# One inverse product for two heads in a chunked RWKV-7 chain, and output rows finished one by one

## The chip, the core and the metric

The kernel runs on one core of a Trainium2 chip. The metric is the device time of one execution in microseconds (us). The profile is that of one profiled execution; its span covers the instructions that the profiler saw.

The engines are named as in the profile: PE is TensorE (matrix products), PEld its weight loads, DVE is VectorE, ACT is ScalarE, POOL is GpSimd, and SP issues most transfers. Each engine works through its own instructions in the order of the program. An instruction whose operands aren't ready holds up all that stand behind it on its engine.

## What is computed

One layer of a sequence model on 512 tokens of 1024 channels: three token mixers (a short convolution, a gated linear recurrence, and an RWKV-7 state recurrence of 16 heads of 64), merged by gates, then an MLP with a squared ReLU, and a final normalization. The part that the change touches:

```python
def step(state, inp):
    r_t, w_t, k_t, v_t, kk_t, a_t = inp
    sa = jnp.einsum('bhvk,bhk->bhv', state, -kk_t)
    state = (state * w_t[:, :, None, :]
             + sa[..., None] * (kk_t * a_t)[:, :, None, :]
             + v_t[..., None] * k_t[:, :, None, :])
    y_t = jnp.einsum('bhvk,bhk->bhv', state, r_t)
    return state, y_t
...
def rms_norm(x, g):
    xf = x.astype(jnp.float32)
    y = xf * lax.rsqrt(jnp.mean(xf * xf, axis=-1, keepdims=True) + EPS)
    return (y * g.astype(jnp.float32)).astype(x.dtype)
...
return rms_norm(x, final_g)
```

## The kernel before

All weights and activations are split into a high and a low part, and each dense product is three matrix products (`mm3`, L163 to L165, shown in the profile as `pp`, `p` and `acc`). These dense products are most of the work of PE.

The recurrence runs in 8 chunks of 64 tokens for 4 groups of 4 heads. A group goes through these steps: `krv` (projections and decays), `amat` (the matrices within a chunk, L471 and L482, tiles pA and pB), `inverse` (the inverse of a unit triangular 64x64 matrix for each of 32 pairs of head and chunk, kept as TT in the tile Z, L490 to L537), `chain` (the 8 chunks one after another, L538 to L607), and `post_norm` (the per-head normalization of the result Y, with the row transposes pYt, L627).

The four heads of a group have two numbers: h, the half of the 128 partitions of a state tile in which the head lies, and jj, the column block. `HEADS` is the order in which the (jj, h) pairs are issued. One chunk of the chain does this:

1. pu <- sv, AXt (L563): four products, one for each head. For the four heads they give the right-hand sides u0, which ACT copies from PSUM to the tile u (L566, L567).
2. pu <- u, Z (L571): four products of 64 rows, 64 columns and 64 outputs, the inverse of each head times u0. All four inverses lie in partitions 0 to 63, and so does u0.
3. py <- St, RT (L578): four 64x64 products of the carried state; not in the first chunk of a group, which has no state yet.
4. DVE copies the solution to sv (L585, L586); then come pS <- sv, BKT (L593, the new state) and py <- sv, AXt (L578, the output).

Between these dependent steps PE works on the dense projections of the next stage ("fill"). The generator functions of the chain and of the fill are woven by `weave` (L752): chain steps get a higher priority by an offset, and the scheduler then sets the final order of each engine's instructions. `pin` keeps the products of a set together. The last group has as its fill the rest of the projections and the first half of the output projection. In that group `open_m` (L807 and on) also loads earlier merge results (mh, ml) on POOL's queue.

After the four groups come the rest of the output projection, the two MLP products, and the end: `last(i)` (L973 to L999) runs the last two blocks of the second MLP product for row tile i (128 tokens, two halves of 512 channels), adds the residual (DVE, `stt`), sums the squares (ACT), multiplies by the final gain (POOL, L983), takes the square root and reciprocal, scales by it (L992 on ACT, L994 on DVE) and sends the half out. `last` is a generator with one stop before the scaling; the order of the calls is 0, 1, 2, 0, 1, 3, 3, 2, so that rows 0 and 1 are scaled after row 2's evictions, and row 2 after row 3's.

Of the kernel before, what the change touches and what calls it, by code (L numbers as in the profile page):

```python
# [9 lines left out]
F32 = mybir.dt.float32  # L10
F32R = mybir.dt.float32r
I32 = mybir.dt.int32
AF = mybir.ActivationFunctionType
# [5 lines left out]
P = 128  # L19
# [10 lines left out]
S = 512  # L30

AL, ALM = 256, 2048
D = 1024
KT = 8
NG = 4
NC = 8
L = 64
# [15 lines left out]
HEADS = ((0, 1), (0, 0), (1, 1), (1, 0))  # L53
# [40 lines left out]
def block_kernel(ctx, tc, xt, win, par, mulr, sw, wout, w1, w2, fg, cst, eyes, out):  # L94
    nc = tc.nc
    v, ac, gp, pe, sy = nc.vector, nc.scalar, nc.gpsimd, nc.tensor, nc.sync
# [4 lines left out]
    def stt(o, a, s, b, op0, op1):  # L101
        return v.scalar_tensor_tensor(out=o, in0=a, scalar=s, in1=b, op0=op0, op1=op1)  # L102
# [64 lines left out]
    def pin(first, mm):  # L167

        if first:
            tc.keep_in_program_order(mm)  # L170
# [106 lines left out]
    mld = dp.tile([6, P, S], F32R, name="mld")  # L277
    smk = sp.tile([P, S], F32, name="smk")
# [209 lines left out]
    def inverse(G_):  # L488
# [37 lines left out]
        for half in range(2):  # L526
            pg = pm.tile([P, 16, 32], F32, tag="pm", name="pT")
            for i in range(16):
                l = 16 * half + i
                pin(i == 0, pe.matmul(pg[0:32, i], gs[32:64, l], TT[32:64, l, 32:64], start=True, stop=True))  # L530
            ac.copy(TT[0:32, 16 * half:16 * half + 16, 32:64], pg[0:32])
            yield
        for h in range(2):
            ac.copy(AXt[0:64, 2 * h:2 * h + 2, :, 0],
                    G_.AR[64 * h:64 * h + 64, :, :, 0])
        G_.TT = TT
        G_.inv_done = True  # L537

    def chain(G_, c_lo, c_hi):
# [5 lines left out]
        for c in range(c_lo, c_hi):  # L545
# [19 lines left out]
            u0 = sp.tile([64, 4, L], F32, tag="u0", name="u0", bufs=1)  # L565
            ac.copy(u0[:, 0:2], pu[0:64, 0:2])  # L566
            ac.copy(u0[:, 2:4], pu[64:128, 0:2])  # L567
            yield
            for jj, h in HEADS:
                e = 2 * h + jj  # L570
                pin(e != 2, pe.matmul(pu[64 * h:64 * h + 64, 2 + jj], TT[:, e * 8 + c], u0[:, e],  # L571
                                      start=True, stop=True))
# [4 lines left out]
            def out_mm(w, x, h, jj, first, last, behind):  # L577
                mm = pe.matmul(py[64 * h:64 * h + 64, jj], w, x, start=first and jj == 0, stop=last,  # L578
                               skip_group_check=True)
                pin(behind or (jj, h) != HEADS[0], mm)  # L580

# [3 lines left out]
            v.tensor_copy(sv[0:64, 0:2], pu[0:64, 2:4])  # L585
            v.tensor_copy(sv[0:64, 2:4], pu[64:128, 2:4])  # L586
# [220 lines left out]
    G_ = GS[NG - 1]  # L807
# [101 lines left out]
    with tc.tile_pool(name="mw", bufs=2) as mw, \  # L909
# [41 lines left out]
        with tc.tile_pool(name="fin", bufs=1, side="right") as fin:  # L951
# [21 lines left out]
            def last(i):  # L973
                ss = fin.tile([P, 2], F32, tag="fss", name="fss", bufs=2)
                x3f = xr[:, i] if i < 3 else fin.tile([P, D], F32, name="x3f")
                for h in range(2):
# [6 lines left out]
                    (v if (i, h) == (3, 0) else gp).tensor_tensor(out=x3f[:, hs], in0=xr[:, i, hs], in1=fgt[:, hs], op=MUL)  # L983
                sd = fin.tile([P, 2], F32, tag="fsd", name="fsd", bufs=2)
# [3 lines left out]
                yield  # L988
                for h in range(2):
                    hs = slice(h * S, (h + 1) * S)  # L990
                    if h == 0 and i != 2:
                        ac.activation(x3f[:, hs], x3f[:, hs], AF.Copy, scale=sd[:, 0:1])  # L992
                    else:
                        v.tensor_scalar(out=x3f[:, hs], in0=x3f[:, hs], scalar1=sd[:, 0:1], scalar2=None, op0=MUL)  # L994
                    (ac if h == 0 and i != 2 else sy).dma_start(out[i, :, hs], x3f[:, hs])

            gens = [last(i) for i in range(4)]
            for i in (0, 1, 2, 0, 1, 3, 3, 2):
                next(gens[i], None)  # L999
# [75 lines left out]
```

## Time and profile before

| | us |
|---|---|
| median of 3 runs (lowest, highest) | 1125.88 (1125.72, 1127.33) |
| the profiled execution's own time | 1126.26 |
| its span | 1124.5 |
| busy: ACT | 519.2 (46%) |
| busy: POOL | 58.9 (5%) |
| first product of the chain in group 1 begins | 347.27 |
| last product of PE begins | 1114.60 |
| last output transfer issued | 1120.95 |

A row of the timeline is: start, duration, engine, line, operation, output tile <- input tiles, the tile shape on PE (rows x columns of the array), the operand's shape, and how many records are in the row. A matrix product of the types used here is two records in the profile. A square bracket at the end names the idle time before the row and what ended it. L numbers are lines of the kernel before, unless the text says otherwise; L99 to L105 are helper functions of DVE, so that tile names tell more than these lines.

### The profile page before, as it was taken

To read this page: it belongs to the slowest core of one execution; us is meant where nothing else is said; L and a number is where in the kernel's file an instruction comes from. 1 tells how busy PE (TensorE), PEld (TensorE's weight loads), DVE (VectorE), ACT (ScalarE), POOL (GpSimd) and SP (SyncE) were. 2 spreads that over 40 slices of the span, in tenths; PEclk is the share of its full clock that TensorE was granted. 3 is DMA by queue.
4 is the path that set the end of the run, shared out by engine and by line. 5 is a ranking of instruction groups with operands and counts; after the bars stand their busy time and mean duration, and the time that the engine had idled before them with its cause. 6 is when DMAs were issued, how large, how long until landed. Compare 5 with 4: busy or idle time off the path is not lost.

```text
span 1124.5 us, 16256 instructions
## 1 busy us (share of the span) xinstructions
PE 1087.3 (97%) x6396; PEld 869.7 (77%) x6396; DVE 766.3 (68%) x1369; ACT 519.2 (46%) x837; POOL 58.9 (5%) x99
## 2 busy tenths in 40 slices
PE   8899989999989999989999989999999999999996
PEld 5677867778867678867678867898888888888885
DVE  7998995989986889975888967686444443222224
ACT  6655355534457534456534474564344333112113
POOL 2200000000000000000000020100000000000003
PEclk8999997999999999999999999999999999999998
DMA  6232222231233131232231262455322225322222
GB/s 212 71 103 80 73 74 77 62 103 57 90 117 99 58 103 57 89 120 88 61 95 65 85 206 85 171 180 161 109 95 94 94 94 191 105 98 94 93 94 75
DMA packets 37772, 114.60 MB, mean 102 GB/s; under 512 B 4544, under 2 KB 8128, under 8 KB 37696
## 3 DMA queue, kind: packets, MB, share of 16 engines
q1 hardware_dynamic: 30768, 95.48, 26.6%
q0 software_dynamic: 6352, 17.30, 4.5%
q8 instruction: 50, 0.82, 0.3%
q10 hardware_dynamic: 576, 0.79, 0.2%
q14 instruction: 26, 0.21, 0.1%
HBM read 104.64 MB, written 8.91 MB: 101 GB/s over the span
## 4 chain that ended last, share of the span: by engine, by line
PE 71%; DVE 22%; issue 3%; ACT 2%; DMA 1%; SPq 0%; ACTq 0%; DVEq 0%
PE pp L163 8%; PE pp L164 8%; PE pp L165 8%; PE acc L165 6%; PE acc L164 6%; PE acc L163 6%; PE p L164 5%; PE p L165 5%; PE p L163 5%; DVE wlo L99 5%; DVE dg L99 4%; DVE Z L99 3%; PE pA L471 2%; DVE u L102 2%; PE py L578 2%
## 5 line engine op out<-in xcount | busy, mean ns | idle before, releaser
L99 DVE TENSOR_TENSOR wlo<-raw,whi 128x1024 fp32r<-128x1024 f32 (+1 forms) x172 | 209.4, 1218 | 215.7 <-ACT whi L142 213.6
L142 ACT CAST whi<-raw 128x1024 fp32r<-128x1024 f32 (+1 forms) x172 | 178.1, 1036 | 286.1 <-PE acc L165 125.7
L165 PE MATMUL pp<-hh,wlo 128*128 128x512 f32 x696 | 278.0, 401 | 5.8 <-DVE wlo L99 5.8
L164 PE MATMUL pp<-hl,whi 128*128 128x512 f32 x696 | 278.3, 400 | 3.9 <-DVE hl L102 3.9
L163 PE MATMUL pp<-hh,whi 128*128 128x512 f32 x696 | 278.5, 401 | 1.4 <-DVE ks L102 0.6
L165 PEld LDWEIGHTS pp<-hh,wlo 128*128 128x128 f32 x696 | 131.9, 190 | 34.4 <-DVE wlo L99 7.3
L163 PEld LDWEIGHTS pp<-hh,whi 128*128 128x128 f32 x696 | 132.0, 190 | 31.9 <-ACT u L664 2.1
L164 PEld LDWEIGHTS pp<-hl,whi 128*128 128x128 f32 x696 | 132.0, 190 | 31.6 <-DVE hl L102 4.7
L165 PE MATMUL p<-h2h,wlo 128*128 128x512 f32 (+1 forms) x264 | 101.2, 383 | 0.0
L163 PE MATMUL p<-h2h,whi 128*128 128x512 f32 (+1 forms) x264 | 101.1, 383 | 0.0
L164 PE MATMUL p<-h2l,whi 128*128 128x512 f32 (+1 forms) x264 | 101.0, 383 | 0.0
L163 PE MATMUL acc<-whi,ah 128*128 128x512 f32 x256 | 99.6, 389 | 0.0
L164 PE MATMUL acc<-wlo,ah 128*128 128x512 f32 x256 | 99.6, 389 | 0.0
L165 PE MATMUL acc<-whi,al 128*128 128x512 f32 x256 | 99.6, 389 | 0.0
L165 PEld LDWEIGHTS p<-h2h,wlo 128*128 128x128 f32 x264 | 49.6, 188 | 9.7
L163 PEld LDWEIGHTS p<-h2h,whi 128*128 128x128 f32 x264 | 49.6, 188 | 9.7
L164 PEld LDWEIGHTS p<-h2l,whi 128*128 128x128 f32 x264 | 49.6, 188 | 9.5
L165 PEld LDWEIGHTS acc<-whi,al 128*128 128x128 f32 x256 | 48.0, 188 | 10.1
L164 PEld LDWEIGHTS acc<-wlo,ah 128*128 128x128 f32 x256 | 48.0, 188 | 10.1
L163 PEld LDWEIGHTS acc<-whi,ah 128*128 128x128 f32 x256 | 48.0, 188 | 9.8
L99 DVE TENSOR_TENSOR Z<-Z,dg 64x31 f32<-64x31 f32 (+15 forms) x124 | 42.2, 340 | 4.1
L99 DVE TENSOR_TENSOR dg<-Z 64x31 f32<-64x31 f32 (+15 forms) x124 | 42.2, 340 | 4.1
(299 smaller groups left out, 1533.8 us busy)
## 6 DMA issues: line engine op xcount, KB each, us to landing
raw<-in_win SPq DMA_DIRECT2D x88, 512.0 KB, 3.5
raw<-in_w SPq DMA_DIRECT2D x64, 512.0 KB, 3.5
raw<-in_wout SPq DMA_DIRECT2D x16, 512.0 KB, 3.5
swr<-in_sw SPq DMA_DIRECT2D x16, 128.0 KB, 2.1
x2T<-in_xt POOLq DMA_DIRECT2D x4, 512.0 KB, 7.1
x2d<-st POOLq DMA_DIRECT2D x8, 256.0 KB, 2.6
xr<-x2d POOLq DMA_DIRECT2D x1, 2048.0 KB, 9.1
xT<-in_xt SPq DMA_DIRECT2D x3, 512.0 KB, 6.7
```

The lines of the kernel that those rows point to most:

```text
L99: return v.tensor_tensor(out=o, in0=a, in1=b, op=op)
L102: return v.scalar_tensor_tensor(out=o, in0=a, scalar=s, in1=b, op0=op0, op1=op1)
L142: ac.copy(hi[:, sl], raw[:, sl])
L163: pe.matmul(ps, wh, xh, start=start, stop=False)
L164: pe.matmul(ps, wh, xl, start=False, stop=False)
L165: pe.matmul(ps, wl, xh, start=False, stop=stop)
L471: pe.matmul(pts[h][:, ci], G_.BK[rows, jj, c], G_.AR[rows, jj, c], start=True, stop=True)
L578: mm = pe.matmul(py[64 * h:64 * h + 64, jj], w, x, start=first and jj == 0, stop=last, skip_group_check=True)
```

## The change

It has three parts.

**The inverse product.** The heads of one jj (h = 0 and h = 1) are put into one product. The inverse of h = 0 stays in partitions 0 to 63, the inverse of h = 1 is copied to partitions 64 to 127 by a transfer inside the on-chip memory on POOL's queue (64 partitions of 4 KB, one per group). The right-hand sides are written as blocks beside zeros: two tiles of 128 x 2 x 2 x 64, zeroed once at the start, take u0 of h in partitions 64h and columns 64h. A product with 128 rows, 64 outputs and 128 columns then gives both heads' solutions beside each other. Two such products for each chunk stand in place of four of 64 x 64 x 64.

**The order of heads.** `HEADS` starts with jj = 1 and puts both h of one jj next to each other; the first product of py follows it.

**The end.** The stop in `last` goes, and the four rows are called one after another. Of each row the first half is multiplied by the gain on POOL and scaled on ACT; the second half is done in one DVE instruction (x times reciprocal times gain) and sent by SP.

```diff
-HEADS = ((0, 1), (0, 0), (1, 1), (1, 0))
+HEADS = ((1, 0), (1, 1), (0, 0), (0, 1))
...
+    u0s = [sp.tile([P, 2, 2, L], F32, name=f"u0{i}") for i in range(2)]
+    for t in u0s:
+        gp.memset(t, 0.0)
...
+        Zf = Z.rearrange("p a b c -> p (a b c)")[:, 0:1024]
+        gp.dma_start(Zf[64:128].rearrange("p (l t) -> p l t", t=L), TT[:, 16:32])
...
-        G_.TT = TT
+        G_.TT = Zf.rearrange("p (j c t) -> p j c t", j=2, c=NC)
...
-            u0 = sp.tile([64, 4, L], F32, tag="u0", name="u0", bufs=1)
-            ac.copy(u0[:, 0:2], pu[0:64, 0:2])
-            ac.copy(u0[:, 2:4], pu[64:128, 0:2])
+            u0 = u0s[c % 2]
+            for h in range(2):
+                ac.copy(u0[64 * h:64 * h + 64, :, h], pu[64 * h:64 * h + 64, 0:2])
             yield
-            for jj, h in HEADS:
-                e = 2 * h + jj
-                pin(e != 2, pe.matmul(pu[64 * h:64 * h + 64, 2 + jj], TT[:, e * 8 + c], u0[:, e],
-                                      start=True, stop=True))
+            for jj in (1, 0):
+                pin(jj == 0, pe.matmul(pu[64 * jj:64 * jj + 64, 2:4].rearrange("p h v -> p (h v)"), TT[:, jj, c],
+                                       u0[:, jj].rearrange("p h v -> p (h v)"), start=True, stop=True))
...
-                mm = pe.matmul(py[64 * h:64 * h + 64, jj], w, x, start=first and jj == 0, stop=last,
+                mm = pe.matmul(py[64 * h:64 * h + 64, jj], w, x, start=first and jj == HEADS[0][0], stop=last,
...
-            v.tensor_copy(sv[0:64, 0:2], pu[0:64, 2:4])
-            v.tensor_copy(sv[0:64, 2:4], pu[64:128, 2:4])
+            for jj in range(2):
+                v.tensor_copy(sv[0:64].rearrange("p (h j) v -> p h j v", j=2)[:, :, jj], pu[64 * jj:64 * jj + 64, 2:4])
...
             def last(i):
...
-                    (v if (i, h) == (3, 0) else gp).tensor_tensor(out=x3f[:, hs], in0=xr[:, i, hs], in1=fgt[:, hs], op=MUL)
-                sd = fin.tile([P, 2], F32, tag="fsd", name="fsd", bufs=2)
+                x0, x1 = xr[:, i, 0:S], xr[:, i, S:D]
+                o0 = x0 if i < 3 else fin.tile([P, S], F32, name="x3f")
+                gp.tensor_tensor(out=o0, in0=x0, in1=fgt[:, 0:S], op=MUL)
                 tt(sd[:, 0:1], ss[:, 0:1], ss[:, 1:2], ADD)
                 ac.activation(sd[:, 1:2], sd[:, 0:1], AF.Sqrt, bias=epst[:, 0:1], scale=1.0 / D)
                 v.reciprocal(sd[:, 0:1], sd[:, 1:2])
-                yield
-                for h in range(2):
-                    hs = slice(h * S, (h + 1) * S)
-                    if h == 0 and i != 2:
-                        ac.activation(x3f[:, hs], x3f[:, hs], AF.Copy, scale=sd[:, 0:1])
-                    else:
-                        v.tensor_scalar(out=x3f[:, hs], in0=x3f[:, hs], scalar1=sd[:, 0:1], scalar2=None, op0=MUL)
-                    (ac if h == 0 and i != 2 else sy).dma_start(out[i, :, hs], x3f[:, hs])
-
-            gens = [last(i) for i in range(4)]
-            for i in (0, 1, 2, 0, 1, 3, 3, 2):
-                next(gens[i], None)
+                stt(x1, x1, sd[:, 0:1], fgt[:, S:D], MUL, MUL)
+                sy.dma_start(out[i, :, S:D], x1)
+                ac.activation(o0, o0, AF.Copy, scale=sd[:, 0:1])
+                ac.dma_start(out[i, :, 0:S], o0)
+
+            for i in range(4):
+                last(i)
```

How the scheduler now orders the engines is seen at three places. First PE in group 1, from the first chunk's right-hand sides on (L563 before, L570 after) to its inverse product (L571 before, L578 after). L163 to L165 (L164 to L166 after) are fill.

```order
L563 MATMUL pu<-sv,AXt 64x64 x4
L164 MATMUL pp<-hl,whi 128x512
L165 MATMUL pp<-hh,wlo 128x512
L163 MATMUL pp<-hh,whi 128x512
L571 MATMUL pu<-u_3078,Z 64x64 x4
```

Now there are twelve fill products between them in place of three:

```order
L570 MATMUL pu<-sv,AXt 64x64 x4
L165 MATMUL pp<-hl,whi 128x512
L166 MATMUL pp<-hh,wlo 128x512
L164 MATMUL pp<-hh,whi 128x512
L165 MATMUL pp<-hl,whi 128x512
L166 MATMUL pp<-hh,wlo 128x512
L164 MATMUL pp<-hh,whi 128x512
L165 MATMUL pp<-hl,whi 128x512
L166 MATMUL pp<-hh,wlo 128x512
L164 MATMUL pp<-hh,whi 128x512
L165 MATMUL pp<-hl,whi 128x512
L166 MATMUL pp<-hh,wlo 128x512
```

The next rows are one fill product and the new inverse product, `L578 ... 64x128 x2`. The same nine products more stand at this place in all four groups, and are missing from the fill later in the chain: in the last group 22 products fewer stand ahead of the first pYt.

Second, PE at the next chunk of the same group, which has a carried state: the inverse product and what follows it, before.

```order
L571 MATMUL pu<-u_3135,Z 64x64 x4
L578 MATMUL py<-St,RT 64x64 x4
L404 MATMUL pn<-bh,bd 128x512
L550 MATMUL pV<-ident,v_1510 128x128
L550 MATMUL pV<-ident,v_1511 128x128
```

And the same place in the changed kernel:

```order
L408 MATMUL pn<-bh,bd 128x512
L578 MATMUL pu<-u_221,Z 64x128 x2
L585 MATMUL py<-St,RT 64x64 x4
L557 MATMUL pV<-ident,v_1512 128x128
L557 MATMUL pV<-ident,v_1513 128x128
```

The state's products still follow the inverse product directly, but the two sets no longer have the same tile shape on the array: 128 rows x 64 columns, then 64 x 64.

Third, DVE at the end of the kernel, before: `xr<-acc` are evictions, `fsd<-fss` sums the two halves' squares, L994 scales.

```order
L102 SCALAR_TENSOR_TENSOR xr_8535<-acc,sc_8527,xr_8535 128x512
L99 TENSOR_TENSOR fsd<-fss 128x1
L983 TENSOR_TENSOR x3f<-xr_8535,fgt 128x512
L987 RECIPROCAL fsd<-fsd 128x1
L102 SCALAR_TENSOR_TENSOR xr_8535<-acc,sc_8527,xr_8535 128x512
L994 TENSOR_SCALAR xr_8535<-xr_8535,fsd 128x512 x2
L99 TENSOR_TENSOR fsd<-fss 128x1
L987 RECIPROCAL fsd<-fsd 128x1
L994 TENSOR_SCALAR x3f<-x3f,fsd 128x512
```

The changed kernel, from the evictions of row 2's second half and row 3's first half on; `xr<-xr,fsd,fgt` is the new instruction for the second half of a row:

```order
L103 SCALAR_TENSOR_TENSOR xr_8447<-acc,sc_8439,xr_8447 128x512 x2
L996 RECIPROCAL fsd<-fsd 128x1
L103 SCALAR_TENSOR_TENSOR xr_8447<-xr_8447,fsd,fgt 128x512
L100 TENSOR_TENSOR fsd<-fss 128x1
L103 SCALAR_TENSOR_TENSOR xr_8447<-acc,sc_8439,xr_8447 128x512
L996 RECIPROCAL fsd<-fsd 128x1
L103 SCALAR_TENSOR_TENSOR xr_8447<-xr_8447,fsd,fgt 128x512
L100 TENSOR_TENSOR fsd<-fss 128x1
L996 RECIPROCAL fsd<-fsd 128x1
L103 SCALAR_TENSOR_TENSOR xr_8447<-xr_8447,fsd,fgt 128x512
```

Between row 3's last eviction and its sum there now stand one reciprocal and one piece of row 2, where two scalings stood.

On POOL's queue the new transfer (`DMA Z<-Z 64x1024`) stands, in the last group, behind three pairs of the loads of mh and ml that `open_m` issues, and ahead of two more pairs.

More of the change, by code (lines that the diff above doesn't have):

```diff
@@ L974, in last @@
                 ss = fin.tile([P, 2], F32, tag="fss", name="fss", bufs=2)
[L975 removed]
+                sd = fin.tile([P, 2], F32, tag="fsd", name="fsd", bufs=2)
                 for h in range(2):
```

## The prediction

> **What bounds the kernel now.** I read the page's table of engines first, then its chain of work, then the windows of the chain stages, then the waits of PE, and last the timeline of PE around one chunk.
>
> ```profile
> PE 1087.3 (97%) x6396; PEld 869.7 (77%) x6396; DVE 766.3 (68%) x1369; ACT 519.2 (46%) x837; POOL 58.9 (5%) x99
> ...
> PE 71%; DVE 22%; issue 3%; ACT 2%; DMA 1%; SPq 0%; ACTq 0%; DVEq 0%
> ```
>
> PE is busy for 97% of the span and carries 71% of the chain; no other engine passes 68%. The chain stages of two head groups, as windows (window, span, then sum and count of PE, PEld, DVE, ACT, POOL, granted clock, DMA share, GB/s), say the same of the place that changes:
>
> ```profile
> 360.00:400.00 40.00, 40.00 (x331) 28.76 (x330) 36.06 (x83) 23.83 (x50) 1.58 (x3) 1.00 0.22 67
> 530.00:560.00 30.00, 30.00 (x280) 20.78 (x280) 26.37 (x66) 18.09 (x42) 0.11 (x1) 1.00 0.21 62
> ```
>
> PE never stops there and the clock is full, so in the chain a part is worth exactly what it puts on or takes from PE's stream. Waits of others behind it cost nothing unless PE runs out of fill. PE's waits, the two that matter below:
>
> ```profile
> PE pT L530 <- ACT dg L524: 4.8, 1, 4.8
> ...
> PE pYt L627 <- DVE Y L99: 0.2, 1, 0.2
> ```
>
> **The inverse product on PE.** The group rows give the old form, and the timeline gives a chunk without and one with the carried state (start, duration, then x records; a matmul of these types is two records).
>
> ```profile
> L571 PE MATMUL pu<-u,Z x256: 218/218/366, 177.9 to 726.7; 64*64 64x64 f32 x128
> ```
> ```profile
> 348.21 0.40 PE L163 MATMUL pp<-hh,whi 128*128 128x512 f32 x1
> 348.54 0.45 PE L571 MATMUL pu<-u,Z 64*64 64x64 f32 x8
> 348.92 0.50 PE L164 MATMUL pp<-hl,whi 128*128 128x512 f32 x1
> 349.25 0.39 PE L165 MATMUL pp<-hh,wlo 128*128 128x512 f32 x1
> 349.48 0.40 PE L163 MATMUL pp<-hh,whi 128*128 128x512 f32 x1
> ```
> ```profile
> 365.57 0.27 PE L571 MATMUL pu<-u,Z 64*64 64x64 f32 x2
> ...
> 365.85 0.40 PE L578 MATMUL py<-St,RT 64*64 64x64 f32 x5
> 366.18 0.50 PE L163 MATMUL pp<-hh,whi 128*128 128x512 f32 x1
> ```
>
> Full products follow each other by 0.23 us (349.25 to 349.48). The eight records of chunk 0: the last began at 348.54 + 0.45 - 0.22 = 348.77, so seven steps took 0.23, 0.033 each, in two column halves side by side. From 348.21 to 349.25 pass 1.04 us; two full products (0.46) and eight steps (0.26) explain 0.72. The other **0.32 us is the price of one visit** to a smaller tile shape: 0.10 on the way in (0.33 for 0.23), about 0.12 on the way out (348.77 to 348.92 for 0.033), 0.10 on the product after it (348.92 to 349.25). In the chunk with state, sixteen records take 365.57 to 366.18 = 0.61 against 0.38 (348.54 to 348.92) for eight: RT's products add 0.23 = 8 x 0.029, their own steps and no more, because they stand in the same 64x64 shape as the inverse product before them.
>
> Now the new form. Two products of 128 rows and 128 columns replace four of 64 and 64: four records, in the same two column halves. That streams as many columns as before (4 x 128 beside 8 x 64). Half the records go, and with them at most a few ns each: I take 0.015 us saved per chunk, bounds 0 to 0.05. So **the gain that a halved count suggests isn't there**. But the tile is now 128x64, and RT's products behind it in the order are still 64x64: 28 of the 32 chunks (all but each group's first, which has no state) get one shape change that was not there.
>
> No row shows 128x64 followed by 64x64. The nearest is a change between two shapes of equal row depth or width, pA to pB:
>
> ```profile
> L471 PE MATMUL pA<-AR,BK x256: 272/272/374, 96.0 to 594.6; 64*128 64x128 f32 x128
> ```
> ```profile
> 255.19 1.16 PE L471 MATMUL pA<-AR,BK 64*128 64x128 f32 x8 [0.19 <-DVE AXt L99]
> 256.27 0.66 PE L482 MATMUL pB<-ident,BK 128*128 128x128 f32 x4
> ```
>
> The last pA record began at 255.19 + 1.16 - 0.27 = 256.08; the seven before took 0.127 each, and pB came 0.19 later: a change of 0.06. From above: half of a whole visit, 0.16; the way out and the next product together, as the worst, 0.22. From below: 0, if 128x64 and 64x64 with one column width can share the array. I take **0.12**, the way out of a small shape with the next record at its normal step, between 0.06 and 0.16. Net 0.12 - 0.015 = 0.105 per chunk, x 28 = **+2.9 us** (-0.4 at no change, +5.7 at 0.22). Chunk 0, four times: -0.06.
>
> The Trainium skill, page "TensorEngine Tiling (Array Packing)", section "Key Properties", says that a change of the tiling mode, as against a change of tile within it, drains the TensorE. The trace agrees where it can be seen: 0.32 us for a visit, and none between the inverse product and RT in one shape. By that rule the new pair pays, which speaks against this change; a rule without a drain would leave the -0.4.
>
> **What feeds the product.** The u0 copies on ACT and the sv copies on DVE are as many and as long as before, and PE has no wait for either in the chain. The inverse of the second head pair now goes through one more DMA per group, 256 KB on POOL's queue, and PE must not come to it too early. The order puts nine more fill products between a group's first product and its inverse product: 9 x 0.23 = 2.1 us. In group 1:
>
> ```profile
> 345.79 0.58 ACT L531 COPY Z<-pT 32x512 f32<-32x512 f32 x1 [0.44 <-PE pT L530]
> ...
> 347.27 0.45 PE L563 MATMUL pu<-sv,AXt 64*64 64x64 f32 x8
> ```
> ```profile
> DMA to landing us min/median/max: 3.2/3.3/3.9
> ```
>
> The last copy that the DMA waits for ends at 346.37. A transfer of the same size and queue into the same tile lands 3.2 to 3.9 us after its issue, so at 349.6 to 350.3. PE reached the product at 348.54 and now comes 2.1 us later, at 350.6. Hidden, by 0.3 to 1 us. The last group is tighter: the DMA stands on POOL behind six loads of 256 KB.
>
> ```profile
> 667.35 1.04 ACT L531 COPY Z<-pT 32x512 f32<-32x512 f32 x2
> ...
> 671.00 0.45 PE L571 MATMUL pu<-u,Z 64*64 64x64 f32 x8
> ```
> ```profile
> ml<-mld POOLq DMA_DIRECT2D x5, 256.0 KB, 4.9
> ```
>
> Copy's end 668.39, landing after 3.3 (alone) to 4.9 (as those loads): 671.7 to 673.3; PE comes at 671.00 + 2.1 = 673.1. I put 0, bounds 0 to 0.5 for each group. What is queued behind the waiting DMA on POOL are stores of mh, ml and in the last group two pairs of loads that arrive some 0.6 us later; they are needed by the fill only at the end of the group. The nine fills are taken from the end of the chains: in the last group the row transposes pYt stand 22 rows (5.1 us) earlier behind the work on Y:
>
> ```profile
> 697.10 0.69 DVE L99 TENSOR_TENSOR Y<-Y,gst 128x512 f32<-128x512 f32 x1
> ```
>
> Y was done at 697.8 and pYt began at 703.7 in the tile's own list, 5.9 ahead: 0.8 remain. At the second half PE waited 0.2 (above), and there the order gives 20 rows more. I put 0, bounds -0.2 to +1. In the prologue the order shifts a few products by some rows around stalls that stay; 0, bounds -1 to +1.
>
> **The tail.** After PE's last product DVE sets the end:
>
> ```profile
> 1114.97 0.74 DVE L102 SCALAR_TENSOR_TENSOR xr<-acc,sc,xr 128x512 f32<-128x512 f32 x1
> 1115.64 0.80 DVE L99 TENSOR_TENSOR fsd<-fss 128x1 f32<-128x1 f32 x1
> 1116.36 0.68 DVE L983 TENSOR_TENSOR x3f<-xr,fgt 128x512 f32<-128x512 f32 x1
> 1116.96 0.15 DVE L987 RECIPROCAL fsd<-fsd 128x1 f32<-128x1 f32 x1
> 1117.04 0.73 DVE L102 SCALAR_TENSOR_TENSOR xr<-acc,sc,xr 128x512 f32<-128x512 f32 x1
> 1117.69 1.88 DVE L994 TENSOR_SCALAR xr<-xr,fsd 128x512 f32<-128x512 f32 x2
> 1119.49 0.15 DVE L99 TENSOR_TENSOR fsd<-fss 128x1 f32<-128x1 f32 x1
> ```
> ```profile
> 1114.60 0.39 PE L165 MATMUL acc<-whi,al 128*128 128x512 f32 x1
> ```
> ```profile
> 1120.95 0.34 ACTq L995 DMA_DIRECT2D out<-x3f  x1
> ```
>
> Row 3's add at 1119.49 stood behind two scalings of row 2; from it to the last issue pass 1.46 us of square root, reciprocal, scaling, and this piece stays. What changes is when the add comes. The new order between the eviction of row 3's first half (1114.97) and that add: eviction 0.70, reciprocal 0.1, second half of row 1 0.70, add 0.15, eviction 0.70, reciprocal 0.1, second half of row 2 0.70, together 3.15 against 4.52: **-1.4**. Against it: the adds and the new three-operand pieces read two SBUF tiles while POOL multiplies, and adds of 128x1 took 0.80 beside it and 0.15 alone; one such loss of 0.65 gives -0.7. And for it: the first half could be evicted from 1113.6 on (a half's products, 6 x 0.23, before PE's end at 1115.0), up to 1.3 earlier. Bounds -2.7 to 0; I take **-1.2**.
>
> The Trainium skill, page "SBUF — State Buffer", section "Who interferes with whom", has the port that VectorE and GpSimd share as an exclusive lock for a whole instruction. The 0.80 beside the 0.15 agrees; by that rule three new pieces can each wait out a POOL multiplication, and the tail's gain would be 0 rather than 1.2.
>
> **Sum**: 2.9 - 0.06 - 1.2 = **+1.7 us** on the profiled execution's 1126.26 (1124.5 of span and 1.8 around it). That execution lies 0.4 above the median of the runs, 1125.88; put on the median, as the changed kernel will be measured, it gives **1127.6**, 0.15% slower. A measurement of this kernel tells about 0.2% from no change, 2.25 us: 1123.6 to 1128.1.
>
> **Rivals.** (a) *No price between two shapes of one column width*: -0.4 - 1.2 = -1.6, so 1124.3. For it: the column halves stay the same, and the way in and out is paid already; against it pA to pB at 0.06. (b) *The change costs a full half visit or more*, 0.16 to 0.22: 28 x 0.145 to 28 x 0.205 = 4.1 to 5.7, less 1.2: +2.9 to +4.5, 1128.8 to 1130.4, slower than before. It decides the sign at 0.14 per change, (2.25 + 1.26) / 28 + 0.015. For it: all three parts of the visit are in the rows; against it: only one change is added, and RT's records are short. (c) *The DMA takes the place of a wait*: it lands after PE has used up its fills. At 0.5 to 1 us in each of four groups +2 to +4 on the sum, 1129.6 to 1131.6. For it the last group's 0.2 us; against it the 0.3 to 1 us elsewhere. A stall near 4.8 would cost more:
>
> ```profile
> 169.30 3.62 PE L530 MATMUL pT<-Z,dg 32*32 32x32 f32 x64 [4.78 <-ACT dg L524]
> ...
> 176.91 0.63 PE L165 MATMUL pp<-hh,wlo 128*128 128x512 f32 x1
> 177.34 0.63 PE L163 MATMUL pp<-hh,whi 128*128 128x512 f32 x1
> ```
>
> After it, products follow by 0.43 instead of 0.23 (176.91 to 177.34). The fills leave no room for so long a wait. (d) *The tail brings nothing*: the new pieces of rows 1 and 2 each wait for a POOL multiplication and lose the 0.65 that the add lost, 1.3 of the 1.4; 1128.8. (e) *The reordering helps where I put 0* (prologue, pYt, a shorter tail): 1123 to 1125.
>
> **Chances.** Forecast (1126.3 to 1128.6) 0.45; (a) 0.2; (b) 0.15; (c) 0.08; (d) 0.06; (e) 0.06. The range leaves out (c)'s upper half, (b)'s top and (e)'s bottom: 1123.7 to 1130.2. Faster by over 0.2%: half of (e) and a third of (a), 0.12. Slower: (b), (c), (d) and a quarter of the forecast, 0.40. Between: 0.48.
>
> **What would show it.** In the changed kernel's timeline of a chunk: the four records of the inverse product in about 0.2 us, then a step of 0.12 more than usual to RT's first record (a: none; b: 0.16 or more, with RT's own records or the next product late too). PE's waits should have no row for Z at the inverse product (c: one, 0.5 or more, in the last group first). The tail should issue its last DMA 4.8 us after PE's end in place of 6.0. PE's steps of full products in the chain must be 0.23 as before; if they are not, none of this sum holds.

## The result and the profile after

The changed kernel is slower by 0.6%: 1133.03 us (median of 4 runs, 1131.65 to 1135.05) against 1125.8 us for the kernel before beside it. The ratio is 1.0064, with a 95% interval of 1.0052 to 1.0077. In a later series it gave 1135.57 against 1126.88, 1.0074 (1.0053 to 1.0095). The prediction was 1127.6, in a range of 1123.7 to 1130.2: the time lies above the range.

The profiled execution took 1131.65, 5.4 more than that of before, span against span (1129.9 and 1124.5). The page first: engines, then the chain of work.

```profile
PE 1093.0 (97%) x6268; PEld 868.1 (77%) x6268; DVE 763.1 (68%) x1367; ACT 519.0 (46%) x838; POOL 59.0 (5%) x102
...
PE 66%; DVE 22%; issue 7%; ACT 3%; DMA 2%; POOL 0%; SPq 0%; ACTq 0%; DVEq 0%; POOLq 0%
```

PE is the bound as before. It has 128 records fewer (two small products fewer in each of 32 chunks, at two records each; a full product, 128x512, is one record) and is busy for 5.7 us more. Where the time goes is read from windows that begin and end at the same product in both kernels: group 1's chain (first right-hand side to first pYt), the last group to the end of the first MLP product, and two inverse stages (first pA to first right-hand side). Columns: window, its length, PE busy and records, granted clock, DMA share, GB/s. Before:

```profile
347.27:409.86 62.59, 62.59 (x503) 1.00 0.23 72
669.73:940.75 271.02, 270.34 (x1635) 1.00 0.38 125
247.02:347.27 100.25, 95.80 (x565) 1.00 0.29 94
415.41:517.24 101.83, 97.41 (x564) 0.98 0.28 92
```

And after:

```profile
347.26:411.75 64.49, 64.19 (x470) 1.00 0.24 71
672.75:947.24 274.49, 272.55 (x1602) 1.00 0.38 124
247.06:347.26 100.20, 95.81 (x565) 1.00 0.29 94
417.31:517.55 100.24, 95.85 (x565) 1.00 0.30 94
```

Group 1's chain lost 1.9 us, the last window 3.5. Group 2's chain lost 1.9 as well (62.6 to 64.5). Its inverse stage got 1.6 us shorter, with the same instructions: the granted clock was 0.98 before and 1.00 after. Such a gift is also why group 0's chain, which starts behind the long stall of PE near 165, is even 0.15 shorter than before. That chain, before and after:

```profile
175.70:241.47 65.77, 65.50 (x503) 0.95 0.20 59
```
```profile
175.88:241.50 65.62, 65.30 (x471) 0.98 0.21 63
```

By an estimate from these rows, 65.6 us at 0.98 in place of 0.95 are worth some 2 us of PE, about what the other chains lost. The ledger of the profiled execution: chains 1 and 2 +3.8, last window +3.5, chain 0 -0.15, group 2's inverse stage -1.6, group 3's +0.8 (clock 0.96 for 0.98), tail -1.1 (below), the rest +0.2: +5.4.

The set that the prediction spoke of, in the same chain (the state's products now have a row of their own behind the inverse product):

```profile
366.51 0.40 PE L166 MATMUL pp<-hh,wlo 128*128 128x512 f32 x1
366.74 0.40 PE L164 MATMUL pp<-hh,whi 128*128 128x512 f32 x1
367.07 0.44 PE L578 MATMUL pu<-u,Z 128*64 128x128 f32 x4
367.44 0.45 PE L585 MATMUL py<-St,RT 64*64 64x64 f32 x8
367.82 0.50 PE L165 MATMUL pp<-hl,whi 128*128 128x512 f32 x1
```

From the first record to the next full product 0.75 us (367.07 to 367.82), 0.61 before. Summed over the 28 chunks with a state: 20.93 us against 17.13, **+3.80**. PE's waits have rows that they didn't have (us in total, times, longest):

```profile
PE pu L570 <- DVE rqq L103: 0.9, 3, 0.3
...
PE acc L166 <- DVE wlo L100: 0.8, 2, 0.6
PE pu L578 <- DMA Z<-Z: 0.6, 1, 0.6
```

The first is the right-hand side's product, once in each of groups 0 to 2: it waits for copies of the state that stand on DVE behind other work (in group 1 a scan of 1.22 us, then rqq). The third is the new transfer, in the last group alone. Its four landings, least, median and longest; the longest is the last group's:

```profile
DMA to landing us min/median/max: 2.8/3.0/5.0
```

The tail. PE's last product, row 3's last eviction and add on DVE, and the last issue:

```profile
1121.09 0.39 PE L166 MATMUL acc<-whi,al 128*128 128x512 f32 x1
```
```profile
1121.02 1.88 DVE L103 SCALAR_TENSOR_TENSOR xr<-xr,fsd,fgt 128x512 f32<-128x512 f32 x1
1122.82 0.15 DVE L100 TENSOR_TENSOR fsd<-fss 128x1 f32<-128x1 f32 x1
1122.89 0.74 DVE L103 SCALAR_TENSOR_TENSOR xr<-acc,sc,xr 128x512 f32<-128x512 f32 x1
...
1123.73 0.75 DVE L103 SCALAR_TENSOR_TENSOR xr<-xr,fsd,fgt 128x512 f32<-128x512 f32 x1
1124.41 0.16 DVE L100 TENSOR_TENSOR fsd<-fss 128x1 f32<-128x1 f32 x1
```
```profile
1126.22 0.35 ACTq L1000 DMA_DIRECT2D out<-x3f  x1
```

PE ends at 1121.48, the last issue comes 4.74 us later; it was 5.96. From PE's end to the end of the span 8.40 us, 9.47 before: **-1.07**. One of the new pieces took 1.88 instead of 0.75, beside a multiplication on POOL (1121.07, 1.28 us); the other three took 0.75, with no multiplication of POOL beside them.

### The profile page after: what moved, and what is told of

It is laid out like the page before. It is cut to its first block, busy times and chain, and to the rows that moved or that the text cites. A ratio compares the mean times of both kernels' runs of the same rounds, so it can differ in the third digit from the quotient of the medians.

```text
span 1129.9 us, 15984 instructions
## 1 busy us (share of the span) xinstructions
PE 1093.0 (97%) x6268; PEld 868.1 (77%) x6268; DVE 763.1 (68%) x1367; ACT 519.0 (46%) x838; POOL 59.0 (5%) x102
## 4 chain that ended last, share of the span: by engine, by line
PE 66%; DVE 22%; issue 7%; ACT 3%; DMA 2%; POOL 0%; SPq 0%; ACTq 0%; DVEq 0%; POOLq 0%
PE pp L165 8%; PE pp L166 8%; PE pp L164 8%; PE acc L166 5%; PE acc L165 5%; PE acc L164 5%; PE p L166 5%; PE p L165 5%; PE p L164 5%; DVE wlo L100 5%; DVE dg L100 4%; DVE Z L100 3%; PE pA L475 2%; DVE u L103 2%; DVE g L103 1%
## 5 line engine op out<-in xcount | busy, mean ns | idle before, releaser
L166 PE MATMUL pp<-hh,wlo 128*128 128x512 f32 x696 | 279.4, 401 | 5.8 <-DVE wlo L100 5.8
L165 PE MATMUL pp<-hl,whi 128*128 128x512 f32 x696 | 279.6, 402 | 3.0 <-DVE hl L103 2.9
L164 PE MATMUL pp<-hh,whi 128*128 128x512 f32 x696 | 276.7, 399 | 1.6 <-DVE us L100 0.8
L166 PEld LDWEIGHTS pp<-hh,wlo 128*128 128x128 f32 x696 | 132.2, 190 | 34.2 <-DVE wlo L100 7.3
L165 PEld LDWEIGHTS pp<-hl,whi 128*128 128x128 f32 x696 | 132.0, 190 | 32.2 <-DVE hl L103 4.1
L164 PEld LDWEIGHTS pp<-hh,whi 128*128 128x128 f32 x696 | 132.0, 190 | 31.9 <-ACT u L671 1.9
L166 PE MATMUL p<-h2h,wlo 128*128 128x512 f32 (+1 forms) x264 | 101.2, 383 | 0.0
L164 PE MATMUL p<-h2h,whi 128*128 128x512 f32 (+1 forms) x264 | 101.1, 383 | 0.0
L165 PE MATMUL p<-h2l,whi 128*128 128x512 f32 (+1 forms) x264 | 101.0, 383 | 0.0
L164 PE MATMUL acc<-whi,ah 128*128 128x512 f32 x256 | 99.6, 389 | 0.0
L165 PE MATMUL acc<-wlo,ah 128*128 128x512 f32 x256 | 99.6, 389 | 0.0
L166 PE MATMUL acc<-whi,al 128*128 128x512 f32 x256 | 99.6, 389 | 0.0
L165 PEld LDWEIGHTS p<-h2l,whi 128*128 128x128 f32 x264 | 49.6, 188 | 9.7
L166 PEld LDWEIGHTS p<-h2h,wlo 128*128 128x128 f32 x264 | 49.6, 188 | 9.7
L164 PEld LDWEIGHTS p<-h2h,whi 128*128 128x128 f32 x264 | 49.6, 188 | 9.6
L164 PEld LDWEIGHTS acc<-whi,ah 128*128 128x128 f32 x256 | 48.0, 188 | 10.1
L165 PEld LDWEIGHTS acc<-wlo,ah 128*128 128x128 f32 x256 | 48.0, 188 | 10.0
L166 PEld LDWEIGHTS acc<-whi,al 128*128 128x128 f32 x256 | 48.0, 188 | 9.9
```

The costliest lines, as they stand in the source:

```text
L164: pe.matmul(ps, wh, xh, start=start, stop=False)
L165: pe.matmul(ps, wh, xl, start=False, stop=False)
L166: pe.matmul(ps, wl, xh, start=False, stop=stop)
```

## The experiments

Theory: two costs were added in the chain. **Shape**: the change from 128x64 to 64x64 between the inverse product and the state's products. **Displaced fill**: the nine products that the scheduler put ahead of the first inverse product because of the transfer, and the transfer itself. Rivals: the order of heads, the wide product itself, and the tail.

Each run is told by its ratio to the kernel before beside it, and by group 1's chain window, which hardly varies from run to run (64.50 in the changed kernel's second profile, 64.49 in the first). A run's median and its one profiled execution are not the same thing: the windows are of the latter.

**The tail alone** (the kernel before with `last` as in the diff).

> The kernel before with the new tail alone. Theory: the tail gained 1.1 us in the changed kernel (9.51 us from PE's last product to the end of the span before, 8.42 after), so 1.1 less than before: about 1124.7 us. Rival: the tail gains only because other things come late; then no change, 1125.8 us.

Measured 1125.4 us, ratio 0.9997 (0.9987 to 1.0006). In its profile PE's end to the span's end is 8.38 us, 1.09 less than before: the tail's gain is there, alone, and at 0.1% too small for the ratio to show.

**The first chunk on the old products**, so that nothing there waits for the transfer.

```diff
+            if St is None:
+                for jj, h in HEADS:
+                    e = 2 * h + jj
+                    pin((jj, h) != HEADS[0], pe.matmul(pu[64 * jj:64 * jj + 64, 2 + h], G_.TT0[:, e * 8 + c], u0[:, e],
+                                                       start=True, stop=True))
+            else:
                 for jj in (1, 0):
```

> The changed kernel, but the first chunk of each group uses the four old products on partitions 0 to 63, so that nothing of it waits for the new transfer; the order of PE then has 3 fill products before the first inverse product as before, not 12. Theory: the changed kernel loses twice, by the shape change (28 x 0.137 = 3.8 us) and by the nine displaced fill products (waits at the right-hand sides, at the inverse product in the last group, and in the last stage, about 3 us). Here the second goes and the first stays: before + 3.8 - 1.1 for the tail, about 1128.5 us; inverse product to the product behind the state's set still 0.75 us. Rival, only the shape change and the length of the chain count: as the changed kernel, 1132 to 1133 us.

**The state's products in 128 rows**, with zeros for the other head, so that no shape changes inside the set.

```diff
-        G_.RT = sp.tile([P, 2, NC, L], F32, tag="RT", name="RT")
-        ac.copy(G_.RT, G_.AR[:, :, :, 1])
+        G_.RT = RTz
+        for h in range(2):
+            ac.copy(RTz[64 * h:64 * h + 64, h], G_.AR[64 * h:64 * h + 64, :, 1:, 1])
...
-                    out_mm(RT[64 * h:64 * h + 64, jj, c], St[64 * h:64 * h + 64, jj], h, jj, True, False, True)
+                    out_mm(RT[:, h, jj, c - 1], St[:, jj], h, jj, True, False, True)
```

> The changed kernel with the state's products in 128 rows too: RT lies in a tile padded with zeros in the other head's partitions, so these four products have 128 rows x 64 columns like the inverse product ahead of them. The order on PE is that of the changed kernel. Theory of the shape change: the set falls from 0.75 to about 0.61 us in 28 chunks, 3.8 us less than the changed kernel, about 1129 us; the waits stay. Rival, the cost lies in the 128-row product itself or in the order of the heads: the set stays near 0.75 us and the time near 1133 us.

This run, and the later one with both costs out, also have one buffer for u0 in place of two, which the theory doesn't mention.

The first gave 1132.17 (1.0056, 1.0037 to 1.0075), the second 1131.46 (1.0051, 1.0035 to 1.0067): as times they missed the theory by 3.7 and 2.5 us, and neither differs clearly from the changed kernel. The windows say more. Group 1's chain and inverse stage with the old first chunk:

```profile
349.42:412.85 63.43, 63.27 (x475) 1.00 0.25 73
...
246.55:349.42 102.87, 98.68 (x565) 0.97 0.29 91
```

And with the state's products in 128 rows:

```profile
348.92:412.36 63.44, 63.12 (x471) 1.00 0.25 73
...
246.00:348.92 102.92, 98.78 (x565) 0.97 0.29 91
```

Either edit takes some 1.06 us off the chain of group 1, close to what the theory has for that stage (7 x 0.137 for the shape). But in both, group 1's inverse stage took 2.7 us more at a clock of 0.97, for the same number of records: a stretch of low clock that the changed kernel's first profile didn't have. And with the old first chunk the last window is only 0.3 us shorter (274.19 after 274.49), although nothing there waits for the transfer: most of that window's loss has another cause. The set's sum with the state's products in 128 rows is 16.80 us, 4.13 less than 20.93.

**Four products of 64 x 64 with the transfer kept.**

```diff
-            for jj in (1, 0):
-                pin(jj == 0, pe.matmul(pu[64 * jj:64 * jj + 64, 2:4].rearrange("p h v -> p (h v)"), TT[:, jj, c],
-                                       u0[:, jj].rearrange("p h v -> p (h v)"), start=True, stop=True))
+            for jj, h in HEADS:
+                rw = slice(64 * h, 64 * h + 64)
+                pin((jj, h) != HEADS[0], pe.matmul(pu[rw, 2 + jj], TT[rw, jj, c], u0[rw, jj, h],
+                                                   start=True, stop=True))
```

> The changed kernel with the transfer, the heads' order and the tail, but four products of 64 x 64 per chunk again (rows and columns of one head's half each). Theory: no shape change ahead of the state's products, so the set is about 0.61 us and 3.8 us go; the transfer is still waited for in the first chunk, where the four now fall into one and three with nine fill products between (one more visit of 0.3 us in each group): about 1130 us. Rival, the transfer costs little and the shape change all: before - 1.1, about 1125 us.

Measured 1138.84, ratio 1.0113 (1.0092 to 1.0134), far above both. It was a poor experiment: the copies to sv went by h as before, but the new order of heads goes by jj, so the first product of pS needed one copy and the second another, and the scheduler split the set:

```profile
355.65 0.33 PE L601 MATMUL pS<-sv,BKT 128*64 128x64 f32 x2
355.91 0.50 PE L165 MATMUL pp<-hl,whi 128*128 128x512 f32 x1
356.34 0.39 PE L601 MATMUL pS<-sv,BKT 128*64 128x64 f32 x5
```

Each split is one more visit to the small shape. It says that order of heads and copies belong together; it doesn't price the shape. The same with the old order of heads, in which no set is split:

> The changed kernel with its transfer, zero-padded u0 and new tail, but four products of 64 x 64 per chunk in the old order of heads, so that no set is split; twelve fill products stand ahead of the first inverse product as in the changed kernel. No shape change ahead of the state's products. Theory: the 28 x 0.137 go, what the transfer displaces stays: chain stage of group 1 about 63.5 us (62.6 before, 64.5 changed), about 1129 us. Rival, the displaced fill products cost nothing: 62.6 us and about 1125 us.

Measured 1129.86, ratio 1.0038 (1.0024 to 1.0051). No change of shape, twelve fill products: the chain is 0.7 longer than before.

```profile
347.82:411.10 63.28, 63.28 (x502) 1.00 0.26 79
```

The time came out as the theory had it. The wait for the transfer in the last group was longer than the changed kernel's:

```profile
PE pu L579 <- DMA Z<-Z: 1.9, 1, 1.9
```

**Both costs out**: state's products in 128 rows and the old products in the first chunk.

> The changed kernel with both costs of the chain taken out: state's products in 128 rows (no shape change behind the inverse product) and the old products in each group's first chunk (no wait for the transfer, three fill products there as before). Theory: the chain stages of groups 1 and 2 are back at about 62.5 us; the last group's order, with 104 fill products ahead of the last pYt against 84, stays and with it some 2 us; the tail's 1.1 us stay gained: about 1127 us. Rival, the 128-row products are slow by themselves: 63.4 us or more and about 1130 us.

Measured 1128.54, ratio 1.0028 (1.0017 to 1.0039), 1.5 over the theory. The chain is back, and the last window keeps 2.0 us over before, as the theory had it:

```profile
348.36:411.09 62.73, 62.42 (x475) 1.00 0.27 79
671.04:944.03 272.99, 271.93 (x1607) 1.00 0.40 125
```

So group 1's chain: 62.6 (before) and 62.7 with neither cost, 63.4 with the shape change alone (63.3 and 64.0 in two runs below), 63.3 and 63.4 with displaced fill alone, 64.5 with both. The run with 62.7 has the new order of heads: in this chain the order costs some 0.2 us at most.

**The shape change alone, in the kernel before**: RT padded as above, and nothing else.

> The kernel before with one edit: RT lies in a tile padded with zeros in the other head's partitions, so the state's products have 128 rows x 64 columns, behind an inverse product of 64 x 64; the order on PE is that of before. It puts one shape change into the same 28 places and nothing else. Theory of the shape change: the set of inverse and state's products goes from 0.61 to about 0.75 us, 28 x 0.137 = 3.8 us, about 1129.6 us, and the chain stage of group 1 (first right-hand side to first pYt, 62.6 us before) becomes 63.5. Rival, the cost belongs to the 128x128-wide inverse product and not to the change: the set stays at 0.61 us and the time at 1125.9 us.

Measured 1135.8, ratio 1.009 (1.0071 to 1.0109): 10 us, far more than expected. The sets took 21.28 us, +4.15, as expected; 2.8 us were ahead of group 0's first pA, and some in low clock. POOL now zeroed the tile for 1.59 us ahead of its squares of x, but that isn't shown to be the cause: the squares began at 4.30 (4.24 before), and the run above with the state's products in 128 rows zeroes the same tile at the same place and reaches the first pA at 95.91 (95.96 before). Once more, with the zeros written later:

> The earlier run of the kernel before with the state's products in 128 rows also zeroed its padded tile in the prologue, and its first stage grew by 2.8 us. Here the same kernel zeroes it on POOL later, in the first group. Order on PE as before. Theory: the prologue is as before, the 28 sets take 21.2 us together instead of 17.1, and the time is 4 us over before, give or take the clock's low stretches (1 to 3 us), 1128 to 1131 us. Rival, the earlier run's 10 us belong to the products themselves: 1134 us or more.

Measured 1134.89 (1131.08 to 1136.19), ratio 1.0066 (1.0042 to 1.0091). By its median the run came out as the rival had it; the profiled execution, 1131.08, is the fastest of its runs and near the theory's upper bound. The sets are again 21.28 us and the chain of group 1 is 1.4 us longer (0.4 more than the sets explain):

```profile
366.91 0.45 PE L575 MATMUL pu<-u,Z 64*64 64x64 f32 x8
367.29 0.45 PE L582 MATMUL py<-St,RTz 128*64 128x64 f32 x8
367.67 0.50 PE L163 MATMUL pp<-hh,whi 128*128 128x512 f32 x1
```
```profile
348.31:412.30 63.99, 63.93 (x503) 1.00 0.23 68
```

Here the narrow product comes first and the deep ones behind it, and the set grows as in the changed kernel: the price is that of the change, whichever way, and not that of the wide product, which this kernel doesn't have. Why the other runs of this kernel took 2.6 to 5.1 us more than the profiled one stays open, and with it why one of the two costs alone took, in these two kernels, as long as both.

**The transfer replaced by a copy on ACT.**

```diff
-        gp.dma_start(Zf[64:128].rearrange("p (l t) -> p l t", t=L), TT[:, 16:32])
+        ac.copy(Zf[64:128].rearrange("p (l t) -> p l t", t=L), TT[:, 16:32])
```

> The changed kernel with the inverse of the second head pair moved to partitions 64 to 127 by a copy on ACT instead of the transfer on POOL's queue; PE's order has 5 (3 in the last group) fill products ahead of the first inverse product instead of 12. Theory: the 28 shape changes stay, the waits at the right-hand sides and for the transfer go: chain stage of group 1 about 63.5 us (64.5 changed), 1.5 to 3 us less than the changed kernel, about 1130 us. Rival, the twelve fill products were not the cause: 64.5 us and 1133 us.

Measured 1129.69, ratio 1.0023 (1.0012 to 1.0034). The shape change stays, the order on PE is close to before:

```profile
347.96:411.23 63.27, 63.18 (x470) 1.00 0.25 74
672.88:945.45 272.57, 270.66 (x1597) 1.00 0.39 123
```

The chain is 1.2 less than the changed kernel's. The last window is 1.9 less, but it has five records fewer (1597 for 1602): five full products, 1.15 us at 0.23, stand ahead of its start here (284 full products in group 3's inverse stage, 279 in the changed kernel). That leaves about 0.8, of which 0.6 is the wait for the transfer. By the ratio, this one line takes back more than half of the loss.

**The last group alone in the old form.**

> The changed kernel with the last group alone in the old form (four products, no transfer there, u0 without zeros); groups 0 to 2 and the tail as changed. The order in the last group is that of before. Theory: from the last group's first right-hand side to PE's next stage the changed kernel loses about 3.5 us (0.5 to 1 by the shape change, 0.6 by the wait for the transfer, the rest by the order of the last fill products and weight waits), and all of it goes here: about 3.5 us under the changed kernel, 1129.5 us. Rival, this loss comes from the earlier groups' shift against the transfers of the weights: it stays, 1132 to 1133 us.

Measured 1130.58 (1128.21 to 1131.86), ratio 1.0052 (1.0033 to 1.0071): as a time it lies between theory and rival and doesn't differ clearly from the changed kernel. The profiled execution is the fastest of the four; its windows:

```profile
347.14:411.63 64.49, 64.19 (x470) 1.00 0.23 71
672.68:943.79 271.11, 270.40 (x1634) 1.00 0.40 125
```

The whole 3.4 us of the last window go, the chain of group 1 stays at 64.5. The loss there belongs to the last group's own form, and not to its coming later against the weights' transfers.

**No small shape at all**: block-diagonal inverse and state's products over the whole array, two heads each, with an ACT copy and the new tail.

```diff
+            for jj in range(2):
+                pin(jj == 1, pe.matmul(pu[:, 2 + jj], TT[:, jj, c], u0[:, jj], start=True, stop=True))
...
+                for jj in range(2):
+                    pin(True, pe.matmul(py[:, jj], RT[:, jj, c - 1].rearrange("p h t -> p (h t)"), St[:, jj],
+                                        start=jj == 0, stop=False, skip_group_check=True))
```

> A version that draws on the findings: kernel before with the new tail, and inverse and state's products as block-diagonal ones over the whole array (two heads each, 128 rows x 128 columns, 64 vectors), so that this set has no shape change at all; the inverse is brought into blocks by an ACT copy, zeros by POOL, the heads' index order in the tiles is (jj, chunk, h). Theory of the shape change: the set takes 8 records of 0.055 us = 0.45 us with no price of entry and exit, against 1.27 - 0.46 = 0.81 before: 28 x 0.36 + 4 x 0.4 = 11.5 us less in the chain, some of it lost where PE then waits for DVE's copies; with the tail 1112 to 1118 us. Rival, the price of a visit is latency of short products and not of the shape: the chain stage stays at 62 us or more and the time near 1125 us.

Measured 1128.73, ratio 1.002 (1.0006 to 1.0034): no gain. Group 1's chain is 63.27 us, as the rival has it (62 or more), and the time lies over both. The price on entry is gone: the step into the set is 0.23 us, 0.33 before. But the full product behind the set still takes 0.31 to the next (0.33 before) with no change of shape, so that part of a visit's price, some 0.08, isn't the shape's. And the set takes 0.83 us where 0.45 was expected. PE's products and its weight loads of one set:

```profile
363.43 0.57 PE L576 MATMUL pu<-u,Z 128*128 128x64 f32 x4
363.84 0.61 PE L588 MATMUL py<-St,RTz 128*128 128x64 f32 x4
364.26 0.48 PE L416 MATMUL pw<-lws,swah 128*128 128x512 f32 x1
```
```profile
363.35 0.52 PEld L576 LDWEIGHTS pu<-u,Z 128*128 128x128 f32 x4 [0.19 <-ACT u L573]
363.79 0.53 PEld L588 LDWEIGHTS py<-St,RTz 128*128 128x128 f32 x4
```

Loads of whole weights follow each other by 0.11 us (four of 0.19 in 0.52), and the products of 64 vectors go at that pace, not at the 0.055 of their columns. Neither theory nor rival had this. The Trainium skill, "TensorE: Matmul & The Clock Gate", "LDWEIGHTS (loading the stationary operand)", puts a load's time at its columns over 1.2, in ns; for 128 columns that gives an estimate of 107 ns, and the trace's 0.11 us agrees. With the steps into and out of it the set costs 1.37 us, 1.27 before.

**The changed kernel once more.**

> The changed kernel once more, for a second profile: its runs lay 1131.7 to 1135.1 and the first profile was the fastest of them. Theory: chain stages and last stage are the same again (64.5 us in groups 1 and 2), and the spread is in the inverse stages, where PE's granted clock drops after its stalls. Rival: the spread lies in the last group, at the wait for the transfer.

The second profile is of an execution of 1136.56 us, 4.9 more than the first. Chain and last window are the same to 0.01 us; two inverse stages are longer, with the same records and less clock:

```profile
350.46:414.96 64.50, 64.20 (x471) 1.00 0.25 71
677.68:952.16 274.48, 272.61 (x1603) 1.00 0.40 124
248.58:350.46 101.88, 97.40 (x564) 0.98 0.29 92
420.51:522.31 101.80, 97.38 (x565) 0.98 0.29 92
```

Of the 4.9, 3.2 are there and 1.5 ahead of group 0's first pA. Over both series, executions of this kernel at a mean clock of 0.987 took 1131.7 to 1133.2, those at 0.981 to 0.985 took 1134.9 to 1136.6.

No version was faster than the kernel before beyond its interval; the tail alone is level with it.

## Why the prediction was wrong

**The bound** was right: PE's stream sets the time, and full products follow by 0.23 us as before (366.51 to 366.74).

**The inverse product** was right in sign and mechanism, and its size too small. The narrower count saves 0.33 us in 28 chunks (16.80 against 17.13 when no shape changes), 0.012 each for the 0.015 put. The change of shape costs 4.13 / 28 = 0.148 us where 0.12 was put, between the 0.06 and 0.16 of the nearest rows, close to half a visit and just over the 0.14 at which, by the prediction, the change alone makes the kernel slower. The term is 3.8 us instead of 2.9, within its bounds. The Trainium skill's rule, "TensorEngine Tiling (Array Packing)", "Key Properties", that a change of mode drains the TensorE, agrees: there is a price in both directions, 0.148 us. Rival (a), no price between shapes of one column width, fell.

**What feeds the product** is the step that failed. The prediction found the transfer hidden in groups 0 to 2, which it was, by the fill products that the scheduler had placed for it, and then put 0 for taking those nine from elsewhere and for the new order that follows from it. It looked for the loss at the end of the chain, at pYt, where nothing happened (PE waited 0.2 us there again). The loss was inside: the later chunks have their steps closer together, and the right-hand sides' products wait for the state's copies on DVE and ACT. Summed over group 1, the steps from a full product to those products and between them are 0.86 us longer in the changed kernel than before, 0.3 of it as the wait shown above. With displaced fill alone a chain loses 0.7 to 0.85 us, beside the shape change about 1.06 (from 63.43 to 64.49): some 1 us in each of three chains for a term of 0 (in group 0 it lies under the clock's gift).

**The last group** is the other half of the same step: 0 was put there too, and the window lost 3.5 us, where the prediction had 0.8 by the shape change (7 x 0.105). Rival (c) came true in part: the transfer landed after 5.0 us, against an upper bound of 4.9, and PE waited 0.6. Seven changes of shape are 0.95. The rest, some 1.9, is neither. With the old first chunk, so without the wait and the twelve fill products, the window is only 0.3 shorter than in the changed kernel; with a shape change in the old order of products it is only 0.7 longer than before:

```profile
673.59:947.78 274.19, 272.91 (x1606) 1.00 0.40 124
```
```profile
673.88:945.60 271.72, 271.40 (x1634) 1.00 0.39 124
```

Most of it lies late in the window, among the output projection's products (acc) and the transposes of its results (tp, L880 before). 104 full products stand ahead of the last pYt where 84 stood, and the transposes behind it stand in nine places in place of seven. The steps of PE to, from and among the acc and tp there sum to 49.7 us before and 51.4 in the changed kernel, of which 0.8 are waits for weights (wlo). Over all the profiles the sum is 51.4 to 52.0 where the last group has two inverse products a chunk, and 49.0 to 50.2 where it has four, with or without the transfer, the shape change and the twelve fill products. So the new order of the last products costs about 1.8 us here; whether by its places or by its waits wasn't told apart.

**The tail** was right: -1.07 for -1.2, last issue 4.74 us after PE's end for the 4.8 named. One of the new pieces lost to POOL's multiplication (1.88 for 0.75), not three. The exclusive port of the Trainium skill's "SBUF — State Buffer", "Who interferes with whom", agrees with that one, as far as one row can; rival (d), a tail without gain, fell.

**The sum by shown terms**: 3.8 - 1.1 + about 1 in each of three chains + 2.5 beyond the shape change in the last window = 8.2. The two medians give 7.2 and 8.7. The first profile shows 5.4; the clock's terms of the ledger (some -2 in group 0's chain, -1.6 and +0.8 in the inverse stages) make up the difference. That match is an account, and the clock's part was not steered by any run.

**Head order** was not tried alone with copies that fit it; the chain of 62.7 us that has it leaves it some 0.2 us there.

**Smaller points of the working.** The note that a matrix product is two records holds for the small ones alone; no term hangs on it. "22 products fewer ahead of the first pYt" in the last group are those directly ahead of it (43 full products for 65); from the group's first right-hand side on there are 107 in both. And half of 0.06 with a third of 0.2 is 0.10, where the chance of a faster kernel was given as 0.12.

## What to carry to other kernels

A product that streams the same columns in half the instructions gained next to nothing here (0.012 us a chunk), and one that leaves the tile shape of its neighbour pays for the change (0.148 us): look at which shape stands next in the order before counting instructions. Where a scheduler covers a new wait with filler work, that work has been taken from the other waits of the same loop; price it there, even when the new wait itself doesn't show in the trace, and look at what it does to the order of the stage behind. When executions differ by as much as the effect, compare windows between the same two instructions, with the granted clock and the count of records beside them.

## What the hardware showed that was not expected

After two stalls of PE, of 1.3 and 2.4 us, in one inverse stage the clock sometimes dropped and sometimes did not, in the same kernel (1.00 in one 20 us window of the first profile, 0.91 in the same window of the second):

```profile
310.00:330.00 20.00, 16.03 (x68) 1.00 0.41 126
```
```profile
310.00:330.00 20.00, 15.94 (x59) 0.91 0.41 132
```

The Trainium skill, "TensorE: Matmul & The Clock Gate", "What's actually happening", says that the activity window behind the clock runs freely, so that the number of slow products at the start of one kernel differs from run to run. These two profiles agree, for a stretch inside the kernel.

And products with 64 vectors on the whole array went at the pace of the loads of their weights, 0.11 us each, so that filling the array with blocks of zeros cost more than entering and leaving the small shape (1.37 against 1.27 us).
